# FFN input product of a two-layer decoder trunk: four instead of three seven-product blocks per layer, with three of four weight sums made by accumulating DMAs

## The chip, the cores and the metric

One NeuronCore of a Trainium2 chip runs the whole program: two layers over 256 tokens of width 1024, batch 1. The metric is the device time of one execution in microseconds (us), lower is better. Engines are named as in the profile: PE (matmul), PEld (its weight load), DVE (vector), ACT (scalar), POOL, and SP, which only issues DMAs.

## What is computed

Only the feed-forward part of each layer (SwiGLU) is touched. D_MODEL is 1024, FFN_HIDDEN is 2816, all data is float32.

```python
    h = rms_norm(x, ffn_norm)
    gate, up = jnp.split(h @ w_ffn_in, 2, axis=-1)
    return x + (jax.nn.silu(gate) * up) @ w_ffn_out
```

## The kernel before

**Float32 on PE.** Each weight tile `raw` of 128x2048 floats (1 MB, loaded as two DMAs of 512 KB from `wpk`) is split into a high part `wh` (ACT copy to fp32r, in `high`) and a low part `wl` = raw - wh (DVE, in `low`). The activations are split the same way. `mm3` then makes one float32 product of three matmuls of 128x512: high by high, high by low, low by high.

**Slabs.** The FFN's 2816 hidden columns are 11 slabs of 256. Slabs 0 and 1 run first (`slab`). The rest of a layer follows the table `FFN`: `("D", 2), ("Q", 3), ("D", 5), ("Q", 6), ("D", 8), ("Q", 9)`. "D" is one slab by `dense`: 2 weight tiles, 48 matmuls of 512 columns, for both token tiles. "Q" is two slabs by `quad`, a block of seven products in Winograd's form of Strassen's scheme: the two token tiles and the two halves of the 1024 input channels make a 2x2 block matrix of activations; the gate and up columns and the same two channel halves make a 2x2 block matrix of weights 11, 12, 21, 22 (one raw tile each). Seven products of 12 matmuls replace eight. Their operands are sums: S1 to S4 of activations, made once per layer by `quarter_sums`, and T1 to T4 of weights, made for every quad by `difference`, one DVE instruction of 128x2048 each (line 172):

```python
T1 = B12 - B11;  T2 = B22 - T1;  T3 = B22 - B12;  T4 = B21 - T2
```

T1 overwrites the tile of 11, T3 the tile of 12, T2 and T4 share a tile of their own (`T2..q`). PSUM bank qX collects 11, T2, T1 in turn; qY, qV, qZ take 21, 22, T3 and T4.

**The second FFN product.** Each slab's hidden values (256 columns) are transposed (`hidden_T`, tiles `aTT`) and multiplied by one weight tile "fo" (24 matmuls, `fo_all`). Two fo units stand inside each quad, one after each dense slab but the first.

**Order.** `unit_order` makes one list of weight tiles: a quad is the tuple `PRODUCTS` = 11, 21, 22, fo, T2, T3, T1, fo, T4. PE runs it in this order. After each unit, `ahead` calls `staged`, which emits the high part of the unit LOOK = 4 places ahead, the low part of the one 3 ahead, and the weight sum of the one 5 ahead. So ACT and DVE work in a fixed order, some four units before PE. There are 4 raw tiles (`RAWS`), 4 pairs wh, wl (`RING`), and one extra tile (tag `yT`) that takes weight 22 early. All loads are issued by SP, in an order that the scheduler fixes at build time; a load waits until its raw tile is released. POOL issues no load here and does nothing from the end of the layer's constants to the next norm. `later(d, f)` runs `f` after d more units ("ticks"); QUAD_AT sets d for a quad's transposes.

Of the kernel before, what the change touches and what calls it, by code (L numbers as in the profile page):

```python
# [18 lines left out]
P = 128  # L19
# [27 lines left out]
A_AT, B_AT = (1, 8), (1, 3)  # L47
QK_T, IX_T, SC_AT = 4, 4, 1
MT_AT, FI_AT = 3, 3
QUAD_AT = (3, 3)  # L50
WO = ((0, 0, 0), (0, 1, 0), (0, 0, 1), (1, 0, 0), (1, 1, 0), (0, 1, 1), (1, 0, 1), (1, 1, 1))
FFN = (("D", 2), ("Q", 3), ("D", 5), ("Q", 6), ("D", 8), ("Q", 9))
LOOK = 4
PRODUCTS = ("11", "21", "22", "fo", "T2", "T3", "T1", "fo", "T4")
LOADED = {"11": "11", "T1": "12", "21": "21", "22": "22"}
FRONT = ("gA0", "ix")
BLOCKS = ("ak", "aq", "av", "bk", "gA1", "bq", "bv", "gB0", "uA", "gB1", "uB")
# [28 lines left out]
def tile_trunk(ctx, tc, x, angle, wpk, widx, gnorm, gbias, gqk, dlam, subln, const, out):  # L86
# [15 lines left out]
    def b8(shape, name, dt=F32):  # L102
        return pp.tile(shape, dt, name=name, tag="b8", bufs=5)
# [54 lines left out]
    stage = {}  # L158
    diffs = {}

    def difference(n):
        l, name, i = seq[n]
        if n + 1 < len(seq) and seq[n + 1][2] == "T2":
            l, name, i = seq[n + 1][:2] + ("T1",)
        elif name[0] != "q" or i == "T1":
            return
        D = diffs.setdefault((l, name), {})

        def less(new, a, b, to=None):
            a, b = [D[x] if x[0] == "T" else raw_of((l, name, x)) for x in (a, b)]  # L170
            to = {"a": a, "b": b}[to] if to else b8([P, 2048], f"T2{l}{name}")
            nc.vector.tensor_tensor(to, a, b, ALU.subtract)
            D[new] = to

        if i == "T1":
            less("T1", "12", "11", "b")
        elif i == "T2":
            less("T2", "22", "T1")
        elif i == "T3":
            less("T3", "22", "12", "b")  # L180
        elif i == "T4":
            less("T4", "21", "T2", "b")

    def high(n):
        u = seq[n]
        raw = diffs[u[:2]].pop(u[2]) if u[2] in ("T1", "T3", "T4") else diffs[u[:2]]["T2"] if u[2] == "T2" else raw_of(u)
        hi = new_ready(n)[0]
        m = 1 if u[1][0] == "q" and u[2][0] == "T" else 2
        w = 2048 // m
        for k in range(m):  # L190
            nc.scalar.activation(hi[:, k * w:k * w + w], raw[:, k * w:k * w + w], AF.Copy)  # L191
        if u[2] == "11":
            raw_of(u[:2] + ("21",)), raw_of(u[:2] + ("12",))
        stage["raw", n] = raw

    def low(n):
# [1 line left out]
        split[0] += 2  # L198

    def staged(k, end):  # L200
        for fn, m in ((high, k), (low, k - 1), (difference, k + 1)):
            n = max(stage.get(fn, 0), split[0] // 2)
            while n <= min(m, end):
                fn(n)
                n += 1
            stage[fn] = n
# [115 lines left out]
    def quarter_sums(N, banks):  # L322
        name = N["name"]
        f1, f2 = N["f"]
        tiles = [b8([P, 4, 4, P], f"{name}S{h}", F32R) for h in "hl"]
        N["S"] = [[a[:, i] for a in tiles] for i in range(4)]
        s1, s2, s3, s4 = [t2k([P, 512], f"{name}s{i}") for i in range(4)]
        nc.scalar.activation(s4, banks[1], AF.Copy)
        nc.vector.tensor_tensor(s1, banks[0], s4, ALU.add)
        nc.vector.tensor_tensor(s3, f1, banks[0], ALU.subtract)  # L330
        nc.vector.tensor_tensor(s2, s1, f1, ALU.subtract)
        nc.vector.tensor_tensor(s4, f2, s2, ALU.subtract)
        for i, v in ((0, s1), (3, s4), (1, s2), (2, s3)):
            hilo(*N["S"][i], heads(v, 4))

# [415 lines left out]
    for l in range(DEPTH):  # L751
# [195 lines left out]
        def quad(s):  # L947
# [22 lines left out]
            def plus(to, p):  # L970
                return lambda: nc.vector.tensor_tensor(to, to, p, ALU.add)

            def added(to, a, p):
                return lambda: nc.vector.tensor_tensor(to, a, p, ALU.add)

            def silu(t):
                return lambda: nc.scalar.activation(G[t], G[t], AF.Silu)

            def gated(t):
                def f():  # L980
                    nc.vector.tensor_tensor(U[t], G[t], U[t], ALU.mult)
                    later(QUAD_AT[t], lambda: hidden_T(s, t, U[t], range(4)))
                return f

            X = bank(f"qX{name}")
            product(X, A(0, 0), "11", True, [copied(G[0], X)])
            Y = bank(f"qY{name}")
            product(Y, A(0, 1), "21", True, [plus(G[0], Y), silu(0)])
            V = bank(f"qV{name}")
            product(V, S4, "22", True)  # L990
            fo_all()
            product(X, S2, "T2", False, [copied(G[1], X)])
            Z = bank(f"qZ{name}")
# [104 lines left out]
```

## Time and profile before

| | us |
|---|---|
| median of 3 runs (765.39 to 765.80) | 765.46 |
| the profiled execution | 765.12 |
| its span, first to last instruction | 763.4 |
| PE busy | 753.9 (99%) |
| DVE busy | 611.1 (80%) |
| ACT busy | 469.0 (61%) |
| POOL busy | 79.7 (10%) |
| DMA queue q1 (SP's loads), share of 16 engines | 49.6% |
| read from HBM | 136.11 MB |

The FFN of layer 0 lies at about 206 to 400 us, that of layer 1 at about 581 to 760 us. The granted TensorE clock is 1.00 throughout, the 2.4 GHz level. The durations of matmuls in the profile overlap, since PE pipelines them: what one costs is the distance between two starts.

### The profile page before, as it was taken

How to read it: one execution, taken by the hardware profiler on the slowest of the kernel's cores; microseconds unless marked ns; L12 is line 12 of the kernel's file. 1: busy time of each engine (PE TensorE's matmuls, PEld its weight loads, DVE VectorE, ACT ScalarE, POOL GpSimd, SP SyncE). 2: the span in 40 equal slices, each digit the busy share in tenths (PEclk: the TensorE clock that was granted, in tenths of full speed). 3: DMA queues.
4: the chain of work that ended last, by engine and by line, in shares of the span. 5: the costliest groups of instructions: out<-in, count | busy, mean ns of one | idle time of the engine just before them, and what ended most of it. 6: DMA issues, size and time to landing. Idle time of an engine off the chain costs nothing.

```text
span 763.4 us, 10187 instructions
## 1 busy us (share of the span) xinstructions
PE 753.9 (99%) x3638; PEld 617.3 (81%) x3638; DVE 611.1 (80%) x907; ACT 469.0 (61%) x938; POOL 79.7 (10%) x103
## 2 busy tenths in 40 slices
PE   8999999999999999999999999999999999999998
PEld 5878887888888788888888787888888887888886
DVE  4899858768677979979868987667777799797993
ACT  4766596655665655656437676876546656565560
POOL 4741220010030000000011401200001000000000
PEclk9999999999999999999999999999999999999999
DMA  9744635436532752816755273453475227367141
GB/s 302 288 183 166 234 113 181 173 115 231 199 115 104 267 229 110 329 57 224 248 192 221 76 255 125 169 177 124 166 265 205 110 96 280 121 234 263 55 166 55
DMA packets 40452, 137.81 MB, mean 181 GB/s; under 512 B 4897, under 2 KB 5665, under 8 KB 40402
## 3 DMA queue, kind: packets, MB, share of 16 engines
q1 hardware_dynamic: 40320, 136.97, 49.6%
q8 instruction: 28, 0.46, 0.2%
q0 software_dynamic: 80, 0.20, 0.1%
q14 instruction: 22, 0.18, 0.1%
q10 hardware_dynamic: 2, 0.00, 0.0%
HBM read 136.11 MB, written 1.05 MB: 180 GB/s over the span
## 4 chain that ended last, share of the span: by engine, by line
PE 86%; DVE 7%; POOL 2%; issue 2%; DMA 1%; ACT 1%; SPq 0%; ACTq 0%; DVEq 0%
PE fi L238 5%; PE fi L236 5%; PE fi L237 5%; PE fo L237 5%; PE fo L238 5%; PE fo L236 5%; DVE wl L197 3%; PE gB L236 2%; PE gB L238 2%; PE wo L238 2%; PE wo L236 2%; PE gB L237 2%; PE wo L237 2%; PE qX L238 2%; PE qX L237 2%
## 5 line engine op out<-in xcount | busy, mean ns | idle before, releaser
L236 PE MATMUL fo<-wh,aTh 128*128 128x512 f32 (+1 forms) x100 | 38.3, 383 | 0.0
L238 PE MATMUL fo<-wh,aTl 128*128 128x512 f32 (+1 forms) x100 | 38.1, 381 | 0.0
L237 PE MATMUL fo<-wl,aTh 128*128 128x512 f32 (+1 forms) x100 | 38.1, 381 | 0.0
L197 DVE TENSOR_TENSOR wl<-raw1q,wh 128x2048 fp32r<-128x2048 f32 x15 | 34.0, 2284 | 0.6 <-ACT wh L191 0.6
L197 DVE TENSOR_TENSOR wl<-raw0q,wh 128x2048 fp32r<-128x2048 f32 x15 | 34.0, 2284 | 0.6 <-ACT wh L191 0.6
L237 PE MATMUL fo<-wl,aT 128*128 128x512 f32 x80 | 31.4, 392 | 0.6 <-DVE wl L197 0.6
L236 PE MATMUL fi<-wh,f0Th 128*128 128x512 f32 x80 | 31.8, 398 | 0.0
L236 PE MATMUL fi<-wh,f1Th 128*128 128x512 f32 x80 | 31.7, 397 | 0.0
L236 PE MATMUL fo<-wh,aT 128*128 128x512 f32 x80 | 31.5, 394 | 0.0
L238 PE MATMUL fo<-wh,aT 128*128 128x512 f32 x80 | 31.2, 390 | 0.0
L238 PE MATMUL fi<-wh,f0Tl 128*128 128x512 f32 x80 | 31.2, 390 | 0.0
L238 PE MATMUL fi<-wh,f1Tl 128*128 128x512 f32 x80 | 31.2, 390 | 0.0
L237 PE MATMUL fi<-wl,f1Th 128*128 128x512 f32 x80 | 31.2, 390 | 0.0
L237 PE MATMUL fi<-wl,f0Th 128*128 128x512 f32 x80 | 31.1, 389 | 0.0
L191 ACT ACTIVATE wh<-raw0q 128x1024 fp32r<-128x1024 f32 (+1 forms) x24 | 29.1, 1264 | 0.5 <-ACT wh L191 0.5
L191 ACT ACTIVATE wh<-raw1q 128x1024 fp32r<-128x1024 f32 (+1 forms) x24 | 29.1, 1264 | 0.5 <-ACT wh L191 0.5
L191 ACT ACTIVATE wh<-raw1fo 128x1024 fp32r<-128x1024 f32 x22 | 22.1, 1052 | 11.3 <-PE fo L238 6.3
L191 ACT ACTIVATE wh<-raw0fo 128x1024 fp32r<-128x1024 f32 x22 | 22.1, 1052 | 11.1 <-PE fo L238 6.4
L236 PE MATMUL wo<-wh,mTh 128*128 128x512 f32 x64 | 25.6, 400 | 0.0
L197 DVE TENSOR_TENSOR wl<-raw1fo,wh 128x2048 fp32r<-128x2048 f32 x11 | 25.0, 2284 | 0.0
L197 DVE TENSOR_TENSOR wl<-raw0fo,wh 128x2048 fp32r<-128x2048 f32 x11 | 25.0, 2283 | 0.0
L238 PE MATMUL wo<-wh,mTl 128*128 128x512 f32 x64 | 25.0, 391 | 0.0
(1060 smaller groups left out, 2505.0 us busy)
## 6 DMA issues: line engine op xcount, KB each, us to landing
raw0q<-wpk SPq DMA_DIRECT2D x24, 512.0 KB, 5.0
raw1q<-wpk SPq DMA_DIRECT2D x24, 512.0 KB, 5.0
raw0fo<-wpk SPq DMA_DIRECT2D x22, 512.0 KB, 4.6
raw1fo<-wpk SPq DMA_DIRECT2D x22, 512.0 KB, 4.2
raw0fi<-wpk SPq DMA_DIRECT2D x20, 512.0 KB, 4.2
raw1fi<-wpk SPq DMA_DIRECT2D x20, 512.0 KB, 4.1
raw0gA<-wpk SPq DMA_DIRECT2D x8, 512.0 KB, 6.2
raw0gB<-wpk SPq DMA_DIRECT2D x8, 512.0 KB, 4.2
```

The lines of the kernel that those rows point to most:

```text
L191: nc.scalar.activation(hi[:, k * w:k * w + w], raw[:, k * w:k * w + w], AF.Copy)
L197: nc.vector.tensor_tensor(ready[n][1], stage.pop(("raw", n)), ready[n][0].bitcast(F32), ALU.subtract)
L236: nc.tensor.matmul(acc, lhsT=sh, rhs=mh, start=first, stop=False, skip_group_check=more)
L237: nc.tensor.matmul(acc, lhsT=sh, rhs=ml, start=False, stop=False, skip_group_check=more)
L238: nc.tensor.matmul(acc, lhsT=sl, rhs=mh, start=False, stop=last, skip_group_check=more)
```

## The change

The table `FFN` has one dense slab (2) and four quads (3, 5, 7, 9). The quad's signs are turned round so that the weight sums are plain additions: T3 = 12 + 22, T2 = T3 + 11, T1 = 11 + 12, T4 = T2 + 21. The activation sums and the last steps of the quad take the minus signs (`scalar_tensor_tensor` in place of `tensor_tensor`). Of the four sums only T2 stays on DVE. The others are accumulating DMAs, issued by POOL (`more`): the addend is read from HBM and added onto a tile that lies in SBUF, T3 onto the tile of 12, T1 onto the tile of 11, T4 onto the tile of T2, each in two DMAs of 512 KB. The raw tile of 21 is then needed only for its own product, that of 22 too, and 12 has no raw use but T3. Product 22 moves to the end of the quad and accumulates onto qX; bank qV and the DVE step `added` are gone.

```diff
-QUAD_AT = (3, 3)
+QUAD_AT = (3, 2)
...
-FFN = (("D", 2), ("Q", 3), ("D", 5), ("Q", 6), ("D", 8), ("Q", 9))
+FFN = (("D", 2), ("Q", 3), ("Q", 5), ("Q", 7), ("Q", 9))
 LOOK = 4
-PRODUCTS = ("11", "21", "22", "fo", "T2", "T3", "T1", "fo", "T4")
+ADDED = ("q3", "q5", "q7", "q9")
+PRODUCTS = ("11", "21", "fo", "T2", "T3", "T1", "fo", "T4", "22")
...
-        if i == "T1":
-            less("T1", "12", "11", "b")
-        elif i == "T2":
-            less("T2", "22", "T1")
-        elif i == "T3":
-            less("T3", "22", "12", "b")
-        elif i == "T4":
-            less("T4", "21", "T2", "b")
+    def more(to, l, name, x):
+        src, w = where[l, name, x]
+        for j in range(2):
+            nc.gpsimd.dma_start(to[:, j * w:j * w + w], src[j], accum_op=ALU.add)
...
+        if i == "11":
+            D["T3"] = B("12")
+            more(D["T3"], l, name, "22")
+        elif i == "21":
+            D["T2"] = D["T4"] = b8([P, 2048], f"T2{l}{name}")
+            nc.vector.tensor_tensor(D["T2"], D["T3"], B("11"), ALU.add)
+        elif i == "T2":
+            D["T1"] = B("11")
+            more(D["T1"], l, name, "12")
+        elif i == "T1":
+            if name in ADDED:
+                more(D["T4"], l, name, "21")
+            else:
+                nc.vector.tensor_tensor(D["T4"], D["T4"], B("21"), ALU.add)
...
-        nc.vector.tensor_tensor(s1, banks[0], s4, ALU.add)
+        nc.vector.tensor_tensor(s1, s4, banks[0], ALU.subtract)
         nc.vector.tensor_tensor(s3, f1, banks[0], ALU.subtract)
-        nc.vector.tensor_tensor(s2, s1, f1, ALU.subtract)
-        nc.vector.tensor_tensor(s4, f2, s2, ALU.subtract)
+        nc.vector.scalar_tensor_tensor(s2, s1, -1.0, f1, ALU.mult, ALU.subtract)
+        nc.vector.scalar_tensor_tensor(s4, f2, -1.0, s2, ALU.mult, ALU.subtract)
...
-            def gated(t):
+            def gated(t, up):
                 def f():
-                    nc.vector.tensor_tensor(U[t], G[t], U[t], ALU.mult)
-                    later(QUAD_AT[t], lambda: hidden_T(s, t, U[t], range(4)))
+                    nc.vector.scalar_tensor_tensor(U[t], up, -1.0, G[t], ALU.mult, ALU.mult)
+                    later(QUAD_AT[t] - (s + 2 == NFO and t == 0), lambda: hidden_T(s, t, U[t], range(4)))
...
-            V = bank(f"qV{name}")
-            product(V, S4, "22", True)
             fo_all()
...
-            product(X, S1, "T1", False, [copied(U[1], X), added(U[0], U[1], V), gated(0), plus(U[1], Z)])
+            product(X, S1, "T1", False, [copied(U[1], X), plus(U[1], Z)])
             fo_all()
-            product(Z, A(1, 1), "T4", False, [plus(G[1], Z), silu(1), gated(1)])
+            product(Z, A(1, 1), "T4", False, [plus(G[1], Z), silu(1), gated(1, U[1])])
+            product(X, S4, "22", False, [gated(0, X)])
```

How this moves instructions is shown at three places. In the names, `wh` and `wl` are the split weights, `raw0q` a raw tile of a quad in layer 0, `raw0fo` and `raw0fi` those of the second product and of a dense slab, `T20q` the tile of T2 and T4, `g` and `u` the gate and up values, `aT` and `aTl` low parts of transposed hidden values.

DVE, layer 0, the last quad (slabs 9 and 10) of the kernel before, from the low part of 22 to the low part of T4; raw0q_3047 is 22, raw0q_2963 holds T1, raw0q_2973 is 12 and then T3, raw0q_2970 is 21:

```order
L197 TENSOR_TENSOR wl_3051<-raw0q_3047,wh_3050 128x2048
L172 TENSOR_TENSOR T20q_3082<-raw0q_3047,raw0q_2963 128x2048
L276 TENSOR_TENSOR aT_3099<-aTT_3096,aT_3099 128x256
L197 TENSOR_TENSOR wl_3078<-raw0fo_3074,wh_3077 128x2048
L172 TENSOR_TENSOR raw0q_2973<-raw0q_3047,raw0q_2973 128x2048
L971 TENSOR_TENSOR g_3102<-g_3102,qY_3125 128x512
L197 TENSOR_TENSOR wl_3121<-T20q_3082,wh_3120 128x2048
L197 TENSOR_TENSOR wl_3141<-raw0q_2973,wh_3140 128x2048
L197 TENSOR_TENSOR wl_3158<-raw0q_2963,wh_3157 128x2048
L172 TENSOR_TENSOR T20q_3082<-raw0q_2970,T20q_3082 128x2048
L197 TENSOR_TENSOR wl_3177<-raw0fo_3173,wh_3176 128x2048
L197 TENSOR_TENSOR wl_3208<-T20q_3082,wh_3207 128x2048
```

DVE after the change, in the quad of slabs 7 and 8, from the low part of T2 to the T2 sum of the next quad; raw0q_2750 holds T3, raw0q_2769 T1, raw0q_2976 is 22:

```order
L201 TENSOR_TENSOR wl_2859<-T20q_2777,wh_2858 128x2048
L975 TENSOR_TENSOR g_2862<-g_2862,qY_2886 128x512
L280 TENSOR_TENSOR aTl_2907<-aTT_2901,aTh_2906 128x512
L201 TENSOR_TENSOR wl_2881<-raw0q_2750,wh_2880 128x2048
L201 TENSOR_TENSOR wl_2911<-raw0q_2769,wh_2910 128x2048
L201 TENSOR_TENSOR wl_2930<-raw0fo_2926,wh_2929 128x2048
L201 TENSOR_TENSOR wl_2960<-T20q_2777,wh_2959 128x2048
L975 TENSOR_TENSOR u_2865<-u_2865,qZ_2963 128x512
L201 TENSOR_TENSOR wl_2980<-raw0q_2976,wh_2979 128x2048
L180 TENSOR_TENSOR T20q_3011<-raw0q_2984,raw0q_3003 128x2048
```

The rows of line 172 between the low parts are gone but for one, which makes the next quad's T2 (line 180); it now stands behind the low part of 22, and it reads a tile (raw0q_2984) that a DMA of POOL has to finish first.

POOL before, end of the constants for layer 1 and the start of the next norm:

```order
L428 TENSOR_TENSOR sg_2059<-gq_2051,plain 128x5x32 x2
L425 TENSOR_TENSOR cg_2063<-gq_2051,plain 128x320
L428 TENSOR_TENSOR sg_2064<-gq_2051,plain 128x5x32 x2
L271 TENSOR_SCALAR a1r_3382<-a1ss_3366 128x1
L272 TENSOR_TENSOR a1r_3382<-a1r_3382,mhalf 128x1
L271 TENSOR_SCALAR a1r_3432<-a1ss_3402 128x1
```

POOL after, two quads of layer 0 and the start of the next norm:

```order
L165 DMA raw0q_2750<-wpk 128x1024 x2
L165 DMA raw0q_2769<-wpk 128x1024 x2
L165 DMA T20q_2777<-wpk 128x1024 x2
L165 DMA raw0q_2984<-wpk 128x1024 x2
L165 DMA raw0q_3003<-wpk 128x1024 x2
L165 DMA T20q_3011<-wpk 128x1024 x2
L275 TENSOR_SCALAR a1r_3387<-a1ss_3371 128x1
L276 TENSOR_TENSOR a1r_3387<-a1r_3387,mhalf 128x1
```

Each of the new rows is one sum, T3, T1 and T4 in turn; T4's pair (T20q_2777) is followed directly by T3's pair of the next quad (raw0q_2984).

SP before, loads from the second quad of layer 0 (11, 21, 12, two fo) to the next dense slab, with the third quad's 22 (raw0q_3047) ahead of it:

```order
L129 DMA raw0q_2614<-wpk 128x1024 x2
L129 DMA raw0q_2621<-wpk 128x1024 x2
L129 DMA raw0q_2624<-wpk 128x1024 x2
L129 DMA raw0fo_2725<-wpk 128x1024 x2
L129 DMA raw0fo_2824<-wpk 128x1024 x2
L129 DMA raw0q_3047<-wpk 128x1024 x2
L129 DMA raw0fi_2875<-wpk 128x1024 x2
L129 DMA raw0fi_2899<-wpk 128x1024 x2
```

SP after, from the 22 of the second quad (raw0q_2742) over the third quad's 12, 11, 21 and fo to its 22:

```order
L130 DMA raw0q_2742<-wpk 128x1024 x2
L130 DMA raw0fo_2692<-wpk 128x1024 x2
L130 DMA raw0q_2750<-wpk 128x1024 x2
L130 DMA raw0q_2769<-wpk 128x1024 x2
L130 DMA raw0q_2791<-wpk 128x1024 x2
L130 DMA raw0fo_2826<-wpk 128x1024 x2
L130 DMA raw0q_2976<-wpk 128x1024 x2
```

The loads of dense slabs between the quads are gone; quads follow each other with four raw tiles and two fo tiles each, and 12 comes first.

## Rows read from the trace of the kernel before

**Rows 1.** The page, part 1: span, busy us (share), instructions.
```profile
span 763.4 us, 10187 instructions
...
PE 753.9 (99%) x3638; PEld 617.3 (81%) x3638; DVE 611.1 (80%) x907; ACT 469.0 (61%) x938; POOL 79.7 (10%) x103
```

**Rows 2.** Busy time by stretch: two quads of layer 0, then its FFN.
```profile
core 0: us, PE busy (x) PEld busy (x) DVE busy (x) ACT busy (x) POOL busy (x), PEclk, DMA share, GB/s
236.00:264.00 28.00, 27.99 (x124) 22.42 (x123) 26.49 (x17) 16.39 (x19) 0.00 (x0) 1.00 0.39 141
290.00:312.00 22.00, 22.00 (x100) 18.25 (x99) 21.69 (x12) 14.63 (x14) 0.00 (x0) 1.00 0.54 199
...
202.00:380.00 178.00, 177.68 (x810) 146.06 (x809) 155.54 (x124) 108.59 (x132) 6.01 (x9) 1.00 0.51 185
```

**Rows 3.** Timeline of PE, first and last of 36 matmuls without a gap: start, duration.
```profile
206.26 0.39 PE L236 MATMUL fi<-wh,f0Th 128*128 128x512 f32 x1
...
214.19 0.39 PE L238 MATMUL fi<-wh,f0Tl 128*128 128x512 f32 x1
```

**Rows 4.** Timeline of PE, the fo unit in the first quad, layer 0, then layer 1.
```profile
263.60 0.39 PE L236 MATMUL fo<-wh,aT 128*128 128x512 f32 x1
264.30 0.50 PE L237 MATMUL fo<-wl,aT 128*128 128x512 f32 x1 [0.31 <-DVE wl L197]
...
638.91 0.50 PE L237 MATMUL fo<-wl,aT 128*128 128x512 f32 x1 [0.31 <-DVE wl L197]
```

**Rows 5.** Timeline of DVE at the same place.
```profile
261.96 2.28 DVE L197 TENSOR_TENSOR wl<-raw0fo,wh 128x2048 fp32r<-128x2048 f32 x1
264.17 2.28 DVE L197 TENSOR_TENSOR wl<-T20q,wh 128x2048 fp32r<-128x2048 f32 x1
266.46 0.69 DVE L974 TENSOR_TENSOR u<-u,qV 128x512 f32<-128x512 f32 x1
```

**Rows 6.** Groups of DVE by shape, 214 to 383 us: form, count | busy us, mean ns.
```profile
L197 DVE TENSOR_TENSOR wl<-raw0q,wh 128x2048 fp32r<-128x2048 f32 x15 | 34.0, 2284 | 0.6 <-ACT wh L191 0.6
...
L172 DVE TENSOR_TENSOR raw0q<-raw0q,raw0q 128x2048 f32<-128x2048 f32 x6 | 13.7, 2283 | 0.0
...
L172 DVE TENSOR_TENSOR T20q<-raw0q,T20q 128x2048 f32<-128x2048 f32 x3 | 6.9, 2284 | 0.0
```

**Rows 7.** The same view for ACT.
```profile
L191 ACT ACTIVATE wh<-raw0q 128x1024 fp32r<-128x1024 f32 x18 | 18.0, 1051 | 0.5 <-ACT wh L191 0.5
...
L191 ACT ACTIVATE wh<-raw0q 128x2048 fp32r<-128x2048 f32 x6 | 11.1, 1903 | 0.0
```

**Rows 8.** Timeline of PE: the same transpose in the first and second quad.
```profile
269.65 0.27 PE L245 MATMUL aTT<-cst,u 128*128 128x128 f32 x1
...
317.36 0.27 PE L245 MATMUL aTT<-cst,u 128*128 128x128 f32 x1
```

**Rows 9.** DMA, 214 to 383 us: queue (packets, MB, share), issues (KB, us to landing).
```profile
q1 hardware_dynamic: 9031, 31.18, 50.4%
...
raw0fo<-wpk SPq DMA_DIRECT2D x22, 512.0 KB, 4.6
raw0q<-wpk SPq DMA_DIRECT2D x18, 512.0 KB, 5.0
```

**Rows 10.** DMA, first 30 us: the queue of SP, and two loads of 128 KB.
```profile
q1 hardware_dynamic: 3451, 9.23, 88.9%
...
cst<-const POOLq DMA_DIRECT2D x1, 128.0 KB, 5.4
dl<-dlam SPq DMA_DIRECT2D x1, 128.0 KB, 4.1
```

**Rows 11.** Timeline of POOL: a DMA issue, and the first instruction after the FFN.
```profile
1.26 0.79 POOL L351 DMA_DIRECT2D cst<-const  x1 [0.43 <-issue]
...
381.42 0.30 POOL L271 TENSOR_SCALAR a1r<-a1ss 128x1 f32<-128x1 f32 x1 [162.31 <-ACT junk L293]
```

More of the change, by code (lines that the diff above doesn't have):

```diff
@@ L159, in tile_trunk, with sums, B @@
     diffs = {}
-    def difference(n):
+    def more(to, l, name, x):
+        src, w = where[l, name, x]
+        for j in range(2):
+            nc.gpsimd.dma_start(to[:, j * w:j * w + w], src[j], accum_op=ALU.add)
+    def sums(n):
         l, name, i = seq[n]
[L163 to L166, printed above, removed]
         D = diffs.setdefault((l, name), {})
[L169 to L173, printed above, removed]
-        if i == "T1":
-            less("T1", "12", "11", "b")
-        elif i == "T2":
-            less("T2", "22", "T1")
-        elif i == "T3":
-            less("T3", "22", "12", "b")
-        elif i == "T4":
-            less("T4", "21", "T2", "b")
+        def B(x):
+            return raw_of((l, name, x))
+        if i == "11":
[4 more added lines that the diff above has]
+            nc.vector.tensor_tensor(D["T2"], D["T3"], B("11"), ALU.add)
+        elif i == "T2":
+            D["T1"] = B("11")
[5 more added lines that the diff above has]
+                nc.vector.tensor_tensor(D["T4"], D["T4"], B("21"), ALU.add)
     def high(n):
         u = seq[n]
-        raw = diffs[u[:2]].pop(u[2]) if u[2] in ("T1", "T3", "T4") else diffs[u[:2]]["T2"] if u[2] == "T2" else raw_of(u)
+        raw = diffs[u[:2]][u[2]] if str(u[2])[0] == "T" else raw_of(u)
         hi = new_ready(n)[0]
@@ L191, in high @@
             nc.scalar.activation(hi[:, k * w:k * w + w], raw[:, k * w:k * w + w], AF.Copy)
-        if u[2] == "11":
-            raw_of(u[:2] + ("21",)), raw_of(u[:2] + ("12",))
         stage["raw", n] = raw
@@ L200, in staged @@
     def staged(k, end):
-        for fn, m in ((high, k), (low, k - 1), (difference, k + 1)):
+        for fn, m in ((high, k), (low, k - 1), (sums, k + 1)):
             n = max(stage.get(fn, 0), split[0] // 2)
@@ L971, in plus @@
                 return lambda: nc.vector.tensor_tensor(to, to, p, ALU.add)
-            def added(to, a, p):
-                return lambda: nc.vector.tensor_tensor(to, a, p, ALU.add)
             def silu(t):
                 return lambda: nc.scalar.activation(G[t], G[t], AF.Silu)
-            def gated(t):
+            def gated(t, up):
                 def f():
-                    nc.vector.tensor_tensor(U[t], G[t], U[t], ALU.mult)
-                    later(QUAD_AT[t], lambda: hidden_T(s, t, U[t], range(4)))
+                    nc.vector.scalar_tensor_tensor(U[t], up, -1.0, G[t], ALU.mult, ALU.mult)
+                    later(QUAD_AT[t] - (s + 2 == NFO and t == 0), lambda: hidden_T(s, t, U[t], range(4)))
                 return f
```

## The prediction

> **What bounds the kernel now.** I read the page's part 1 first: PE is busy 753.9 of 763.4 us [rows 1], so only what shortens PE's own stream, or makes it wait, can move the time. The windows say the same of the FFN alone: 177.68 of 178.0 us in layer 0, at granted clock 1.00 [rows 2]. A trap lies in the profile's durations. A matmul of 128x512 shows 0.39 us, but 36 of them without a gap start from 206.26 to 214.19, so one costs (214.19 - 206.26) / 35 = 0.2266 us [rows 3].
>
> PE's one loss in an FFN's quads is in the first quad of each layer. There two matmuls of an fo unit start 0.70 us apart instead of 0.23, because DVE's low part wl came late; layer 1 shows the same wait of 0.31 us in the same place [rows 4]. DVE is why: two starts of its 128x2048 instruction lie 2.21 us apart (261.96 and 264.17) [rows 5], and in the quads it is busy 26.49 of 28 and 21.69 of 22 us [rows 2]. So inside a quad DVE is the next bound, right behind PE; the dense slabs in between let it recover. POOL is idle for 162 us of an FFN [rows 11], and the DMA engines work half the time [rows 2, 9].
>
> **PE's work.** Per layer, two dense slabs (96 matmuls) become one quad (84). The hidden transposes stay at 8. Two layers save 24 matmuls: 24 x 0.2266 = 5.44 us, all on PE's stream.
>
> A quad with its two fo units is 84 + 48 = 132 matmuls, 29.9 us. The old period of quad, dense slab and three fo units was 317.36 - 269.65 = 47.71 us [rows 8] for 204 matmuls (46.2 us) and 12 transposes, so one transpose costs PE about 0.12 us and a new quad with its 8 lasts 30.9 us. Four stand back to back, with no dense slab to recover in. That is what every other engine has to keep up with.
>
> **DVE.** Before, one period held 12 low parts and 4 sums, 16 x 2.21 = 35.4 us, and 8 short instructions of the quad at 0.6 to 0.69 (5.2 us), 85% of 47.71 before the dense slab's own short ones. The twelve sums per layer are the groups of six, three and three at line 172, at 2283 ns each like the low parts [rows 6]. Now a quad holds 9 low parts and one sum, 22.1 us, and 7 short ones (one, `added`, goes), 4.8 us: 26.9 of 30.9 us, 87%. With all four sums it would have been 33.5, over the period; so the adds on DMA carry the change. Where DVE failed, the first quad, T1's sum, T3's and T4's are gone from ahead of the late low part: 6.6 us off a lateness of 0.31. I therefore count both stalls as gone, 264.30 - 263.60 - 0.23 = 0.47 us each, 0.94 in all; if they stay, add that back. The turned signs put two `scalar_tensor_tensor` in each layer's activation sums and two in each quad, in place of as many instructions of the same shape: nothing, under PE's matmuls.
>
> **ACT.** Five high parts in halves at 2 x 1.05 us and four whole ones at 1.90 [rows 7] are 18.1 us per quad, and seven short ones at 0.6 make 22.3 of 30.9, 72%: hidden.
>
> **The adds.** 24 sums of 1 MB become 48 DMAs of 512 KB on POOL. No row before shows a DMA that adds, so I bound one from both sides. In 214 to 383 us SP's queue took 50.4% of 169 us for 31.18 MB, 2.73 us per MB, or 1.43 us of all 16 engines per 512 KB [rows 9]. That is the low end: an add that costs what a load costs. The high end is twice that, 2.87 us, since an add has to fetch the tile that it adds onto as well as the addend. In latency a load takes 4.6 to 5.0 us to land [rows 9]; in the first 30 us a load of 128 KB from POOL landed in 5.4 where SP's took 4.1 [rows 10], and POOL spent 0.79 us to issue one [rows 11], so I add 1.3 us for the queue, and the pair lands about 0.8 + 5.0 + 1.3 = 7.1 us after its issue where nothing is in its way.
>
> Per quad, six raw tiles (four of the quad, two fo) are 6.29 MB, 17.2 us of the engines. Three added tiles take 8.6 us at the low end, 25.8 of 30.9 in all (83%); at the high end 17.2, 34.4 in all (111%). Break-even is (30.9 - 17.2) / 6 = 2.28 us per add, 1.6 times a load. The engines can be held near full: in the first 30 us the same queue had 88.9% of them at 26.7 / 9.23 = 2.89 us per MB [rows 10].
>
> Who waits for them: T2's sum on DVE now waits for T3's add, and behind it stand the low parts of 11 and 21; ACT's high part of T4 waits for T4's add, and behind it stand the copy out of qX and the high part of 22; POOL's queue is in order, so T4's pair stands right ahead of the next quad's T3 pair. That is the tightest place. It opens when the low part of T2 is made, at PE's product 11, and closes when the next T2 sum is due, at PE's product T1: 21, fo, T2, T3, T1, or 72 matmuls, 16.3 us. In it fall four adds and three loaded tiles (fo, 12, 11): 10 x 1.43 = 14.3 us at the low end, 4 x 2.87 + 8.6 = 20.1 at the high end. A late T2 sum has cover: PE needs the low part of 11 only after fo, T4 and 22, 48 matmuls or 10.9 us later, of which DVE needs 4.4 for the sum and the low part. T4's high part has 21, fo and T2, 10.9 us, against 7.1.
>
> I take the low end, or near it: what the engines are busy with in a load is moving 4 KB rows into the tile, and an add writes no more rows than a load, while the fetch of the tile goes the other way. It is a choice, not a reading, and it carries the forecast.
>
> The Trainium skill speaks against it. Its page "Collectives: The Full Stack", section "The bandwidth ceiling: the fold count and why AG ≠ RS ≠ AR", says that an add in the DMA engines costs no time in itself, but needs two source reads on one queue and so halves the rate. By that rule an add would be at my high end; no row of this trace has such a DMA to test it.
>
> **Sum.** The profiled execution took 765.12 us, its span 763.4 plus 1.7 around it. 765.12 - 5.44 - 0.94 = 758.7. The median of the runs stands 0.34 above the profiled one: **759.1 us**, 0.8% faster. This case's own range is 758.3 to 761.5, with the stalls kept or a few short waits at its upper end.
>
> **Rivals.** (A) *The DMA engines become the bound, and it is slower.* If an add costs 2.87 us, each quad wants 34.4 us of transfers in 30.9, 3.5 us short, and the tight place is 3.8 short. The first quad of a layer has most of its tiles loaded before, and the cover of about 6.5 us delays the stall, but the shortage comes back with every quad; six quads at 3.6 are 22 us: 781. It decides from 2.28 us per add on. For it: an add must read its target. Against it: DMA share is only half now, and reads and writes need not share a limit. By the rule of the Trainium skill's "Collectives: The Full Stack" quoted above, this is the outcome. (B) *Latency takes the gain back.* The adds have throughput, but a pair behind SP's loads takes over 10.9 us, ACT stands at T4's high part, and PE loses 0.7 to 0.9 us in each of the eight quads: 759.1 + 8 x 0.8 = 765.5, no change. For it: the chain T3, T2, T1 and T2, T4 runs through three queues in order. Against it: four units of lookahead. (C) *DVE is still late*, 87% busy with no dense slab between: the two stalls stay, 760.0, inside the forecast's range.
>
> **How the numbers follow.** Forecast with C 0.66, A 0.20, B 0.10, and 0.04 for what I have not thought of, half on each side. About 0.2%, 1.5 us, is what a measurement of this kernel can tell from no change. Faster: 0.66 and 0.02, and 0.02 of B's lower edge, 0.70. Same: the rest of B, 0.08. Slower: A and 0.02, 0.22. The range runs from 758.3 to 772: it holds the forecast, B and the near edge of A, and leaves out the body of A.
>
> **What would show it.** Right: PE has 24 fewer matmuls, no wait of its own in the quads above 0.3 us, DVE's line 172 groups give way to one of four per layer, DMA share in the quads 0.8 to 0.9, an add's pair lands in 7 to 10 us. Wrong: PE waiting in every quad, from the second on, for a low part of T4 or 11, with DVE or ACT waiting for a POOL DMA before it, DMA share at 0.95 or more there (A) or well below (B).

## The result, and the profile after

The changed kernel takes **769.52 us** (median of 5 runs, 768.28 to 770.66) beside 765.39 of the kernel before in the same comparison: ratio 1.0061, 95% interval 1.0050 to 1.0072. It is 0.6% slower where 0.8% faster was forecast. The time lies inside the range of 758.3 to 772, but by luck: that end of the range was drawn for the near edge of rival A, and neither the forecast nor A's 781 came. The profiled execution took 768.28 us.

The page, span and part 1, and the two queues of part 3 (packets, MB, share of 16 engines):

```profile
span 766.5 us, 10291 instructions
...
PE 749.3 (98%) x3614; PEld 613.5 (80%) x3614; DVE 589.0 (77%) x889; ACT 482.7 (63%) x940; POOL 122.0 (16%) x151
...
q1 hardware_dynamic: 40320, 136.97, 48.2%
q0 software_dynamic: 6992, 25.37, 18.0%
```

Against [rows 1], PE has 24 instructions less, as forecast, and 4.6 us less of busy time, but the span is 3.1 us longer: PE now stands idle for 17.2 us of it instead of 9.5. The windows of the quads of layer 0 show where (busy us of PE, PEld, DVE, ACT, POOL; granted clock, DMA share, GB/s):

```profile
236.00:264.00 28.00, 28.00 (x126) 23.05 (x125) 20.82 (x15) 17.67 (x20) 4.32 (x5) 1.00 0.94 238
264.00:290.00 26.00, 26.00 (x120) 21.37 (x119) 21.74 (x15) 15.76 (x16) 5.24 (x6) 1.00 1.02 293
290.00:321.00 31.00, 28.90 (x125) 23.51 (x124) 25.27 (x17) 20.66 (x21) 5.24 (x6) 0.94 0.98 284
321.00:352.00 31.00, 30.04 (x137) 24.61 (x136) 25.26 (x17) 20.79 (x21) 3.51 (x4) 1.00 0.98 287
```

The DMA share went from 0.39 and 0.54 [rows 2] to 0.94 and more. PE's first loss comes after 290 us, not in the first quad, where the 0.31 us waits of [rows 4] are gone. Whom PE, ACT and DVE wait for, from the waits (us in total, times, longest; PE's of the whole execution, the other two of 214 to 383 us):

```profile
PE aTT L249 <- DVE u L982: 7.4, 4, 2.8
...
DVE wl L201 <- ACT wh L197: 15.7, 6, 4.3
ACT wh L197 <- DMA T20q<-wpk: 11.0, 4, 3.7
```

In the quads PE waits for no weight part. It waits at the hidden transposes (aTT) for a gated u. One such case, followed through four engines in the timeline (start, duration, engine, instruction; in brackets the idle time before it and what ended it; `T20q` holds T2 and then T4):

```profile
279.33 1.76 POOL L165 DMA_DIRECT2D T20q<-wpk  x2 [8.03 <-DVE wl L201]
...
286.11 0.60 ACT L972 ACTIVATE g<-qX 128x512 f32<-128x512 f32 x1 [0.66 <-PE qX L242]
290.25 1.92 ACT L197 ACTIVATE wh<-T20q 128x2048 fp32r<-128x2048 f32 x1 [3.54 <-DMA T20q<-wpk]
...
292.19 2.29 DVE L201 TENSOR_TENSOR wl<-T20q,wh 128x2048 fp32r<-128x2048 f32 x1 [4.08 <-ACT wh L197]
...
303.74 0.69 DVE L982 SCALAR_TENSOR_TENSOR u<-u,g 128x512 f32<-128x512 f32 x1 [0.70 <-ACT g L978]
...
304.49 0.66 PE L249 MATMUL aTT<-cst,u 128*128 128x128 f32 x4 [2.10 <-DVE u L982]
```

T4's pair of adds is issued at 279.33. ACT comes to T4's high part at 290.25 - 3.54 = 286.71, 7.4 us later, and the tile is ready 10.9 us after the issue. DVE stands behind ACT for 4.08 us, and in the 12 us to the gated u it has only 1.2 us of idle time left; 2.1 us of the delay reach PE. The transfers of the same stretch, 214 to 383 us (queues, then issues with the median us to landing):

```profile
q1 hardware_dynamic: 8986, 31.14, 48.2%
q0 software_dynamic: 3456, 12.58, 40.5%
...
raw0q<-wpk SPq DMA_DIRECT2D x26, 512.0 KB, 7.1
...
T20q<-wpk POOLq DMA_DIRECT2D x8, 512.0 KB, 8.3
```

Adds (q0): 0.405 x 169 / 12.58 = 5.44 us of all engines per MB, 2.85 us per add of 512 KB (0.524 MB). Loads (q1): 0.482 x 169 / 31.14 = 2.62 us per MB. An add costs 2.1 times a load. The first pair of a layer, alone on the engines in 219 to 226 us, says the same:

```profile
q0 software_dynamic: 274, 1.05, 83.8%
...
raw0q<-wpk POOLq DMA_DIRECT2D x2, 512.0 KB, 6.3
```

0.838 x 7 = 5.9 us for the pair, 2.93 per add, and 6.3 us from the issue of an add to its landing (the median of the two) with nothing in its way, where the prediction had counted 7.1.

### The profile page after: what moved, and what is told of

It is laid out like the page before. It is cut to its first block, busy times and chain, and to the rows that moved or that the text cites. A ratio compares the mean times of both kernels' runs of the same rounds, so it can differ in the third digit from the quotient of the medians.

```text
span 766.5 us, 10291 instructions
## 1 busy us (share of the span) xinstructions
PE 749.3 (98%) x3614; PEld 613.5 (80%) x3614; DVE 589.0 (77%) x889; ACT 482.7 (63%) x940; POOL 122.0 (16%) x151
## 4 chain that ended last, share of the span: by engine, by line
PE 71%; DMA 12%; DVE 8%; issue 3%; POOL 3%; ACT 2%; SPq 0%; DVEq 0%; ACTq 0%; POOLq 0%
DMA raw0q<-wpk 5%; DMA raw1q<-wpk 5%; PE fo L242 3%; PE fo L240 3%; PE fo L241 3%; PE qX L242 2%; PE qX L241 2%; PE qX L240 2%; PE fi L242 2%; PE fi L240 2%; PE fi L241 2%; PE gB L240 2%; PE gB L242 2%; PE gB L241 2%; DVE wl L201 2%
## 5 line engine op out<-in xcount | busy, mean ns | idle before, releaser
L240 PE MATMUL fo<-wh,aTh 128*128 128x512 f32 (+1 forms) x132 | 51.4, 389 | 0.0
L242 PE MATMUL fo<-wh,aTl 128*128 128x512 f32 (+1 forms) x132 | 50.7, 384 | 0.0
L201 DVE TENSOR_TENSOR wl<-T21q,wh 128x2048 fp32r<-128x2048 f32 x8 | 18.3, 2287 | 14.1 <-ACT wh L197 14.1
L201 DVE TENSOR_TENSOR wl<-T20q,wh 128x2048 fp32r<-128x2048 f32 x8 | 18.3, 2287 | 13.8 <-ACT wh L197 13.8
L242 PEld LDWEIGHTS fo<-wh,aTl 128*128 128x128 f32 x132 | 24.8, 188 | 5.1
L241 PEld LDWEIGHTS fo<-wl,aTh 128*128 128x128 f32 x132 | 24.8, 188 | 4.7
L240 PEld LDWEIGHTS fo<-wh,aTh 128*128 128x128 f32 x132 | 24.8, 188 | 4.5
L165 POOL DMA_DIRECT2D raw1q<-wpk x16 | 14.8, 1067 | 79.7 <-DVE wl L201 73.3
L165 POOL DMA_DIRECT2D raw0q<-wpk x16 | 14.8, 1082 | 72.8 <-DVE wl L201 53.6
L241 PE MATMUL wo<-wl,mTh 128*128 128x512 f32 x64 | 25.0, 390 | 0.0
```

What stands on the lines that cost most here:

```text
L165: nc.gpsimd.dma_start(to[:, j * w:j * w + w], src[j], accum_op=ALU.add)
L201: nc.vector.tensor_tensor(ready[n][1], stage.pop(("raw", n)), ready[n][0].bitcast(F32), ALU.subtract)
L240: nc.tensor.matmul(acc, lhsT=sh, rhs=mh, start=first, stop=False, skip_group_check=more)
L241: nc.tensor.matmul(acc, lhsT=sh, rhs=ml, start=False, stop=False, skip_group_check=more)
L242: nc.tensor.matmul(acc, lhsT=sl, rhs=mh, start=False, stop=last, skip_group_check=more)
```

## The experiments

Names used in the expectations: **P**, the price: an add holds the DMA engines for twice a load; **L**, the latency of POOL's queue and of the chain T3, T2, T4; **V**, DVE and ACT too late without a dense slab; **PL**, formed later: the price works through T4's tile, which becomes ready too late in its chain. Every ratio is to the kernel before in the same comparison.

**e1_plain_loads.** The adds become loads, so the sums T3, T1 and T4 are left out.

```diff
-            nc.gpsimd.dma_start(to[:, j * w:j * w + w], src[j], accum_op=ALU.add)
+            nc.gpsimd.dma_start(to[:, j * w:j * w + w], src[j])
```

> The accumulate is taken off the 48 DMAs of POOL: each now overwrites its tile with the addend, so the three weight sums are left out (T1, T3 and T4 are one tile each), with the same issues, waits and bytes from HBM. Theory P (price: an add keeps the 16 DMA engines busy twice as long as a load, 2.9 us per 512 KB against 1.4, and the quads ran at a share of 0.98 to 1.02): the quad needs 25.8 us of transfers in 30.9, T4's pair lands earlier, PE's 7.4 us of waits go, about 759 us. Theory L (latency: POOL's queue and its chain of waits, whatever is moved): the waits stay, 767 to 770. Theory V (DVE and ACT too late with no dense slab between quads, whatever DMA does): the waits stay too.

757.70 us (0.9911, 0.9898 to 0.9924). DMA, 214 to 383 us:

```profile
q0 software_dynamic: 3456, 12.58, 20.6%
...
T20q<-wpk POOLq DMA_DIRECT2D x8, 512.0 KB, 4.5
```

The same bytes at half the time, 2.77 us per MB, and a T4 tile after 4.5 instead of 8.3 us. No PE wait is left in the quads. A quad lasts 30.9 us, as worked out (T4's pairs are issued at 278.45, 309.33 and 340.19). So PE's, DVE's and ACT's parts of the forecast hold in these quads (V falls), as does POOL's queue by itself (L falls); what the adds cost is 769.5 - 757.7 = 11.8 us.

**e2_t4_on_dve.** T4's sum on DVE.

```diff
-ADDED = ("q3", "q5", "q7", "q9")
+ADDED = ()
```

> T4's sum goes back to DVE (ADDED empty); T3 and T1 stay adds. Theory P: per quad 17.2 + 4 x 2.9 = 28.8 us of transfers in 30.9, share about 0.93; DVE gets 2.2 us more, 29.1 of 30.9. ACT no longer waits for T4's pair, PE's waits at the hidden transposes shrink from 7.4 to 0 to 3 us, 760 to 764 us. Theory V: DVE at 94% is worse, 770 or more. Theory L: T3's and T1's chain remains, 765 to 768.

763.90 us (0.9989, 0.9980 to 0.9998). The engines' share in 264 to 352 us is 0.86, and PE still waits for u, shorter, but longer than the 0 to 3 us that P allowed:

```profile
PE aTT L249 <- DVE u L982: 4.9, 6, 1.0
```

**e3_transposes_later.** All adds, the hidden transposes one or two slots later.

```diff
-QUAD_AT = (3, 2)
+QUAD_AT = (4, 4)
...
-                    later(QUAD_AT[t] - (s + 2 == NFO and t == 0), lambda: hidden_T(s, t, U[t], range(4)))
+                    later(2 if s + 2 == NFO else QUAD_AT[t], lambda: hidden_T(s, t, U[t], range(4)))
```

> The hidden transposes of a quad, where PE waited, are moved one or two units later (d = 4, 4 instead of 3, 2; the last quad of a layer keeps 2, 2); the adds stay as they are. If PE only waited there because the last steps of the quad come 2 to 3 us late (a lateness that is passed on but does not grow), the waits go and the gain shows: 758 to 761. If the DMA engines are short by 3.5 us per quad and the lateness adds up, it comes out at the weight parts instead: 764 to 770, with PE waiting for wl of T4, 11 or 21.

767.48 us (1.0037, 1.0024 to 1.0050). The wait goes from the transposes to product 21's low part:

```profile
PE qY L241 <- DVE wl L201: 4.0, 4, 1.2
...
PE aTT L249 <- DVE u L982: 0.6, 1, 0.6
```

More slack at the place where PE waits gives little: DVE's lost time comes out one product further on. That is the branch that the expectation had named for engines that are short in every quad.

**e4_dense_between.** Three quads per layer with the dense slabs between, as before, and the adds.

```diff
-FFN = (("D", 2), ("Q", 3), ("Q", 5), ("Q", 7), ("Q", 9))
+FFN = (("D", 2), ("Q", 3), ("D", 5), ("Q", 6), ("D", 8), ("Q", 9))
...
-ADDED = ("q3", "q5", "q7", "q9")
+ADDED = ("q3", "q6", "q9")
```

> The adds alone: slabs as before the change (three quads, dense slabs between), with the three sums by DMA. PE's work is that of before. Theory P: a period of 47.7 us holds 9 tiles of loads and 3 of adds, 25.8 + 17.2 = 43 us, share 0.9: no waits in the quads, and the two stalls of 0.47 us in the first quads go with DVE's relief: 764 to 765. Theory L: adds land too late in any arrangement, 766 to 770.

762.82 us (0.9974, 0.9965 to 0.9983), no PE wait in the quads, share 0.91 in 264 to 352 us. With time between them, adds at the high price are covered. It is 1.2 us faster than P's range; that rest has no row.

**e5_t4_on_dve_later** is e2 and e3 together; **e7_t4_first_quad_added** gives the adds back to the first quad of a layer.

```diff
-ADDED = ()
+ADDED = ("q3",)
```

> T4's sums on DVE (as in e2_t4_on_dve) and the hidden transposes one slot later in every quad but the last (as in e3_transposes_later). P (an add occupies the DMA engines twice as long as a load): with a third fewer adds the engines are 85 to 87% busy, as in e2, and the gated u is only a little late, 4.9 us of waits at the transposes in e2, the longest 1.0; one slot of three products later (2.7 us) covers them all: 763.9 - 4.9 = 759.0, between 758.5 and 760. Had e2's waits another cause, DVE's own load (78.9 of 88 us) as in V, they would move to the weight parts, as those of e3 did: 761 to 763.5.

> As e5_t4_on_dve_later, but T4's sum of the first quad of each layer stays with the DMAs (two more adds of 512 KB per layer) and DVE has one sum of 2.2 us less there. P: the first quad's tiles are loaded ahead, before the FFN's matmuls begin, so its shortage comes last, but what it adds to the queue, 5.8 us of engines per layer, is taken from the next quads, which are at 85 to 87%: no PE wait comes of it and the time is that of e5 within 0.7 us. If DVE's load is what still costs e5 something: 0.5 to 1.5 us faster than e5. If the engines have no room even here: 1 to 2 us slower than e5.

e5: 760.24 us (0.9945, 0.9933 to 0.9956), 0.2 above P's range, e7: 760.00 us (0.9944, 0.9930 to 0.9957). With a share of 0.88 in e5 the later transposes do cover the waits for u, unlike in e3; 0.5 us of waits for weight parts are left. Why both stay 2.3 us or more above e1 isn't settled.

**e6_loads_and_copies**, **e8_copies_ahead**, **e10_copies_between.** Plain loads as in e1, and with each pair two copies of 512 KB from HBM to a spare place in HBM, which nobody waits for. Only the order of the four differs: load, copy, load, copy; copy, copy, load, load; load, copy, copy, load. e10's lines:

```diff
         for j in range(2):
+            nc.gpsimd.dma_start(to[:, j * w:j * w + w], src[j])
+            for k in range(2 - 2 * j):
+                nc.gpsimd.dma_start(spare[spared[0]], src[k])
+                spared[0] += 1
```

> Kernel e1_plain_loads (the 48 adds are plain loads, so that the sums T3, T1 and T4 are left out and the output is not the reference's) with one more transfer behind each of the 48: a copy of the same 512 KB from HBM to a spare place in HBM that nothing reads and nothing waits for. No DMA adds anything here, but POOL's queue holds the DMA engines about as long as it does with the adds, if a copy from HBM to HBM costs what a load costs (2.6 us per MB; no row shows one, the run's own queue row will say). P (it is the time of the engines alone): the time of e1, 757.7, goes back to that of the changed kernel, 769.5, between 766 and 773, with the DMA share in the quads at 0.95 or more and PE waiting at the hidden transposes for u. If something else in an add were to blame, its own latency or its exclusive hold of the tile: it stays at 757.5 to 760. If the copies turn out far cheaper or dearer than loads, the share decides what is to be read.

> Kernel e6_loads_and_copies with each pair's two copies put ahead of its two loads instead of each behind its own (sums left out as there, so the output is not the reference's). The bytes and the engines' time are the same as in e6; what changes is that a tile is ready only when its copies and its loads are both through, which is when an add's pair would be ready (some 1.7 us later still, since POOL issues two more DMAs first, at 0.87 us each). Theory PL (what costs is that the tile itself is ready twice the engine time after its issue, with the engines near full): ACT's waits for T4's tile, 4.5 us in e6's first layer against 11.0 in the changed kernel, come back to 9 or more, PE waits at the hidden transposes for u, 765 to 773. Theory P as stated for e6 (the engines' time alone, wherever it falls): the same time as e6, 760.2, within 1.5.

> Kernel e6_loads_and_copies with the order of the four DMAs of a pair changed: load of the first half, both copies, load of the second half (sums left out as there, so the output is not the reference's). In e8_copies_ahead the copies waited for nothing, so they ran ahead of the place in time at which an add may start; here the first load waits for the tile, and the copies and the second load stand behind it in POOL's queue, so that the extra engine time falls where an add's falls and the tile is ready only behind it. PL (the tile ready late by twice the engine time, at the place where an add stands): ACT's waits for T4's tile 9 us or more in layer 0, PE waits at the hidden transposes for u, 763 to 771. If engine time and its place do not matter and it is a property of the adding transfer that no load and no copy has: 757.5 to 760.5, as e6 and e8.

e6: 760.18 us (0.9943, 0.9922 to 0.9964). e8: 757.86 us (0.9913, 0.9899 to 0.9927). e10: **769.23 us** (1.0059, 1.0045 to 1.0072), the changed kernel's time without a single add. The windows of 264 to 352 us, of e6, e8 and e10 in turn:

```profile
264.00:352.00 88.00, 86.27 (x392) 70.89 (x391) 73.67 (x48) 59.19 (x59) 16.92 (x32) 1.00 1.00 393
```

```profile
264.00:352.00 88.00, 88.00 (x401) 72.89 (x400) 76.73 (x50) 60.77 (x60) 15.64 (x30) 1.00 1.01 397
```

```profile
264.00:352.00 88.00, 82.14 (x373) 67.16 (x372) 70.83 (x48) 55.54 (x56) 16.64 (x32) 1.00 0.96 374
```

The share is about the same, and highest where nothing is lost. So P as e6's expectation put it (the engines' time alone, wherever it falls) fell, and e8 seemed to take PL with it. The timeline of POOL tells why it did not. In e8:

```profile
271.03 0.99 POOL L168 DMA_DIRECT2D spare<-wpk  x2
280.06 1.09 POOL L171 DMA_DIRECT2D T20q<-wpk  x2 [8.04 <-DVE wl L207]
281.15 0.99 POOL L168 DMA_DIRECT2D spare<-wpk  x2
284.08 0.56 POOL L171 DMA_DIRECT2D raw0q<-wpk  x1 [1.94 <-issue]
```

The copies meant for one pair wait for nothing and run right behind the pair before it: T4's at 271.03, 9 us ahead of its loads, those of the next pair at 281.15. e8 had not put the cost where an add has it, and e6 half of it (one copy ahead of a tile's second half; ACT waits 4.5 us for T4's tile in layer 0). In e10 the first load holds the copies back, and the second half of the tile stands behind them (POOL's rows, then the waits, ACT's of 214 to 383 us, PE's of the whole execution):

```profile
279.33 0.55 POOL L168 DMA_DIRECT2D T20q<-wpk  x1 [7.71 <-DVE wl L207]
279.86 0.98 POOL L170 DMA_DIRECT2D spare<-wpk  x2
280.84 0.57 POOL L168 DMA_DIRECT2D T20q<-wpk  x1
```

```profile
ACT wh L203 <- DMA T20q<-wpk: 12.2, 4, 4.1
...
PE aTT L255 <- DVE u L988: 9.7, 5, 3.2
```

ACT's waits for T4's tile come back (12.2 us, 11.0 in the changed kernel), and PE's for u with them. So no adding is needed for a loss of this size, and the share alone doesn't make it: tiles that are ready late do. By the waits it is T4's; T3's and T1's are delayed in the same way, so the time by itself doesn't single it out. One reserve: a load and a copy together hold the engines nearly as long as an add (the queue's share in 214 to 383 us is 38.1% in e10, 40.5% in the changed kernel), but 374 to 397 GB/s moved in these runs where the changed kernel moved 288, so a share near 1 doesn't say that nothing more could pass.

**e9_t4_on_pool.** As e5, T4's sum on POOL.

```diff
-                nc.vector.tensor_tensor(D["T4"], D["T4"], B("21"), ALU.add)
+                nc.gpsimd.tensor_tensor(D["T4"], D["T4"], B("21"), ALU.add)
```

> As e5_t4_on_dve_later, but T4's sum is made by POOL's own tensor_tensor instead of DVE. The only rows of POOL's are small: 0.80 us for 160 elements per partition and 1.03 for 320, so by their slope 1.03 + 1728 x 0.00144 = 3.5 us for 2048, against DVE's 2.2. PL and P: the DMA engines have room as in e5 (two adds per quad), DVE has 2.2 us less per quad; PE's small waits of e5 for weight parts (0.5 us in all) go: 758.2 to 760, as e5 or up to 1.5 us faster. If POOL and DVE hinder each other while POOL's sum runs, DVE's instructions beside it grow over 2.3 us and it is 761 or more.

779.62 us (1.0194, 1.0180 to 1.0208): the forecast missed by 20 us, and the branch for POOL and DVE hindering each other came. POOL's timeline:

```profile
246.69 4.63 POOL L188 TENSOR_TENSOR T20q<-T20q,raw0q 128x2048 f32<-128x2048 f32 x1 [10.72 <-PE aTT L249]
```

4.63 us and not 3.5, and DVE's low parts of quad tiles took 2.75 us on the mean instead of 2.28 (from the groups of DVE). PE waited 14.2 us for weight parts.

**e11_t4_two_added.** As e7, with the last quad's T4 sum added by DMA too: `ADDED = ("q3", "q9")`.

> As e7_t4_first_quad_added, with T4's sum of the last quad of each layer given back to the DMAs as well; DVE keeps the two in the middle. The stretch behind the last quad has the DMA engines at 64% in e5 and e7, so there is room for 5.8 us more, but the last quad's transposes stay at two slots, so a late u shows there. If there is room in time too: as e7, 759 to 760.5; if T4's add is late in the last quad as in the changed kernel, where PE waited there: 760.5 to 763.

**759.75 us (0.9932, 0.9918 to 0.9945)**: it beats both kernels.

**e12_t4_last**, **e13_t4_last_later.** All adds; products 22 and T4 change places, on PE and so on ACT and DVE.

```diff
-PRODUCTS = ("11", "21", "fo", "T2", "T3", "T1", "fo", "T4", "22")
+PRODUCTS = ("11", "21", "fo", "T2", "T3", "T1", "fo", "22", "T4")
```

with `QUAD_AT = (3, 3)` in e12 and `(4, 4)` in e13, and two slots in the last quad. **e14_places_of_e12** keeps the order of the changed kernel and puts every transpose where e12 has it:

```diff
-QUAD_AT = (3, 2)
+QUAD_AT = (2, 4)
...
-                    later(QUAD_AT[t] - (s + 2 == NFO and t == 0), lambda: hidden_T(s, t, U[t], range(4)))
+                    later(QUAD_AT[t] - (s + 2 == NFO), lambda: hidden_T(s, t, U[t], range(4)))
```

> The changed kernel, all four added sums by DMA, with the products 22 and T4 of a quad in the other order: ACT's high part of 22 stands ahead of T4's, PE needs T4 one product (12 matmuls, 2.7 us) later, and the transposes of both halves come three slots after their product (two in the last quad). No byte and no DMA is changed, so the engines' time is that of the changed kernel. PL (the late T4 tile is the cause, and ACT standing at it while 22's tile lies ready): ACT's waits for T4's tile were 2 to 3.7 us in the four quads of layer 0, so 2.7 us more and 22's high part done meanwhile leave a wait of at most 1 us: 758.5 to 762, with the DMA share as high as before. If the shortage is one of the engines' throughput, as e3_transposes_later suggests, whose waits moved to the parts of 11 and 21: the wait comes out elsewhere and it is 765 to 769.

> As e12_t4_last with the transposes one slot later still (four; two in the last quad). PL: if e12 still waits at the transposes, this covers it: 758 to 761, and no slower than e12. Throughput: 765 to 769 with the waits at the weight parts.

> The changed kernel with its order of products (T4, then 22), but every hidden transpose at the place on PE that it has in e12_t4_last: behind product 11 of the next quad for the first half, behind 21 for the second. It tells apart the two things that e12 moved at once. PL as e12 was meant (ACT stands at T4's late tile, and DVE behind ACT): the waits of ACT for T4's tile stay at 10 to 15 us in layer 0, DVE still loses 3 to 4.6 us at T4's low part, PE's waits go from the transposes to the low parts of the next products as in e3_transposes_later: 765 to 769. If the places of the transposes made e12's gain: 761 to 763.5.

e12: **762.22 us** (0.9961, 0.9947 to 0.9974). e13: 765.79 us (1.0014, 1.0006 to 1.0023). e14: **773.77 us** (1.0113, 1.0098 to 1.0129). e12 is 0.2 us above PL's range. e12 and e14 have the same DMAs and the same places of the transposes, and are 11.6 us apart at a share of 1.00 and 0.99. e12, 264 to 352 us, and its waits (PE's of the whole execution, ACT's of 214 to 383 us, here and below):

```profile
264.00:352.00 88.00, 86.14 (x388) 70.19 (x387) 73.33 (x48) 58.80 (x59) 14.00 (x16) 1.00 1.00 288
...
ACT wh L197 <- DMA T20q<-wpk: 4.8, 2, 2.6
...
PE qX L241 <- DVE wl L201: 2.5, 3, 1.2
```

and e14's, with one of its waits in the last quad of layer 0:

```profile
264.00:352.00 88.00, 84.11 (x380) 68.44 (x379) 73.16 (x48) 56.88 (x57) 14.00 (x16) 1.00 0.99 287
...
ACT wh L197 <- DMA T20q<-wpk: 11.2, 4, 3.7
...
PE aTT L249 <- DVE u L982: 12.1, 7, 2.7
...
370.25 0.66 PE L249 MATMUL aTT<-cst,u 128*128 128x128 f32 x4 [2.25 <-DVE u L982]
```

In e12 ACT does 22's high part while T4's tile is still on its way, so it stands for 4.8 us instead of 11.2. But the 11.6 us are not the order of ACT's work alone. With 22 last, e14 has one product less than e12 between 22 and the transposes of the first half, which 22 completes, and none at all in the last quad of a layer, where PE stands there for 2.25 and 2.73 us. Its granted clock was lower too, 0.995 to 0.997 in its four runs against 0.999 to 1.000. So e14 missed twice: PE's waits stayed at the transposes, and the time is 4.8 us above its range.

e3 and e13 compare the orders better: both put the transposes of either half four slots after their product (two in the last quad). Their medians are 1.7 us apart (767.48 and 765.79), their profiled executions 0.75 the other way (765.70 and 766.45), though ACT's waits for T4's tile, e3 first, fall by 8.5 us:

```profile
ACT wh L197 <- DMA T20q<-wpk: 14.1, 4, 4.8
```

```profile
ACT wh L197 <- DMA T20q<-wpk: 5.6, 2, 3.1
```

e13 refuted "no slower than e12": 5.9 us of PE waits at weight parts instead of 3.6, and a time in the branch for throughput. Why later transposes cost here isn't settled, and how much of e12's gain on the changed kernel, 7.3 us, is the order and how much the places isn't either.

**e15_t4_last_two_added** is e12 with `ADDED = ("q3", "q9")`.

> e12_t4_last with T4's sum of the two middle quads of each layer on DVE, as in e11_t4_two_added: the order that gives T4 one product more, and 12.6 us per layer less of the engines' time. PL: what e12 still waits, 3.6 us in all at weight parts, goes with the lower share: 757.5 to 760, at least as fast as e11 (759.75). If DVE's extra 2.2 us in the middle quads, or the order itself, costs something: 760 to 762.

759.56 us (0.9939, 0.9926 to 0.9951): with e11 the fastest that computes everything, and not to be told from it.

## Why the prediction was wrong

**PE's work: right.** 24 matmuls went, and with loads in place of the adds the kernel took 757.7 where the sum gave 759.1; the 1.4 us between them have no row.

**The two stalls: right.** No wait stands in the first quads.

**The price of an add: wrong, and the step that carried the sign.** The low end, 1.43 us, was taken "as a choice, not a reading"; it measured 2.85 to 2.93, at the high end of 2.87. With 2.85 for 1.43 the prediction's own sum of a quad is 17.2 + 6 x 2.85 = 34.3 us in 30.9, and the gain of 6.4 us became a loss of 4.1. The argument for the low end, that an add writes no more rows than a load and that the fetch of the tile goes the other way, has nothing left. The rule of the Trainium skill's "Collectives: The Full Stack", section "The bandwidth ceiling: the fold count and why AG ≠ RS ≠ AR" (two source reads, half the rate), is stated there for a ReduceScatter. The trace of these adds agrees with it: 5.44 against 2.62 us per MB.

**Rival A: its price right, its time 12 us too long, its mechanism at most a part.** It made the loss out of throughput: some 3.6 us short in each of six quads, 22 us. By the measured prices a quad wants 6.29 x 2.62 + 3.15 x 5.44 = 33.6 us in 30.9, 2.7 short, and the middle quads of layer 0 do take about that long: T4's pairs are issued at 279.33, 312.52 and 346.18, 33.2 and 33.7 us apart (1.6 of the first by the clock, below). But e10 lost as much at a share of 0.96, without an add, and e12, with the same DMAs and the engines as full, is at 762.2, 4.5 us above e1. On the other side, e3 and e13 kept 9.8 and 8.1 us of loss over e1 with their waits moved to weight parts, as a shortage would have it. So throughput alone doesn't give the 11.8 us, and no run here divides them between the shortage and the late tile. A left out that the engines have slack ahead of the first quad (the share is 0.61 in 214 to 236 us of the changed kernel) and behind the last loads (0.76 in 352 to 383).

**Rival B: the place right, the size wrong.** "ACT stands at T4's high part, and PE loses" is what happened, but through the doubled price and not through latency at a load's price; e1 has the same queue and no wait. PE loses 1.0 to 2.8 us at four of eight quads, not 0.7 to 0.9 at each.

**The cover of T4: the second wrong step.** The 10.9 us were counted from PE's product 11, where the low part of T2 was to be made and T4's pair issued, to ACT's high part of T4 behind product T2. ACT did come there right behind product T2. But DVE makes the low part of T2 later, behind that of fo: product 11 ends at 274.56, where the first matmul of 21 starts, and the low part at 279.04.

```profile
274.56 0.39 PE L240 MATMUL qY<-wh,f0Th 128*128 128x512 f32 x1
...
276.76 2.28 DVE L201 TENSOR_TENSOR wl<-T20q,wh 128x2048 fp32r<-128x2048 f32 x1
```

That leaves 7.4 us from the issue to ACT, 0.3 over the 7.1 forecast, and the tile took 10.9; PE's product T4 itself never waited. The list of who stands behind the tile named the copy out of qX and 22's high part, but not DVE. DVE stood for 4.08 us behind ACT, and with 87% to do (which the prediction had) it didn't win that back within 12 us. What came late was the gated u, for which the prediction had no cover worked out at all. e10, which loses as much with such a late tile and no add, shows that this path is enough for a loss of this size.

**Rival C, DVE late by itself:** didn't come; DVE is busy 76.7 of 88 us in e1's quads (its window of 264 to 352 us), near the forecast 87%, and PE doesn't wait.

**"What would show it":** the share of 0.95 or more came true, as did waits of ACT, and of DVE behind it, for a DMA of POOL, but PE waiting in every quad for a low part of T4 or 11 didn't; the wait stood at the transposes.

The profiled executions of the changed kernel and of e1 are 768.28 - 757.89 = 10.4 us apart. Of these, 7.4 are PE's waits for u, and 1.6 a clock that fell behind the first of them (below); the other 1.4 have no row. The medians are 11.8 us apart, and the five runs of the changed kernel stand in the order of their mean granted clock: 768.28 at 0.998, 768.82 at 0.996, 769.52 and 770.06 at 0.995, 770.66 at 0.994. So the median run lost more by the clock than the profiled one.

## What to carry to other kernels

Price a new kind of transfer at its dearer bound until a run has shown it, and then don't stop at the share of the engines: two kernels with the same transfers (e8 and e10), at a share of 1.01 and 0.96, were 11.4 us apart, and the one with the higher share was the faster. Follow the tile to the first engine that takes it up in order, not only to the matmul that needs it last; count from when its issue can really start, and count what stands behind that engine. Here the second engine in the chain was near full, and what it lost stayed lost. Of the two ways out, taking some of the adds away (e11, 759.75, with later transposes) gained more than giving the late tile more time (e12, 762.2, where the order and the places of the transposes changed together), and both at once (e15, 759.56) no more than the first.

## What the runs showed of the hardware

An adding DMA from HBM into SBUF took 2.1 times the engines' time of a load (5.44 against 2.62 us per MB) and 0.88 us to issue on POOL (1.76 for the pair at 279.33), where a plain load there took 0.55 (e10's rows above).

PE's granted clock fell behind the 2.10 us wait in layer 0 of the changed kernel, once PE had started again. Windows and two matmul starts:

```profile
304.00:306.00 2.00, 1.51 (x9) 1.35 (x10) 2.00 (x2) 2.00 (x4) 0.49 (x1) 0.99 0.74 135
306.00:308.00 2.00, 2.00 (x7) 1.54 (x6) 2.00 (x4) 1.88 (x2) 0.00 (x0) 0.50 1.08 199
308.00:310.00 2.00, 2.00 (x7) 1.60 (x6) 2.00 (x2) 0.49 (x1) 0.00 (x0) 0.66 0.99 197
...
305.90 0.58 PE L241 MATMUL qX<-wl,f0Th 128*128 128x512 f32 x1
...
309.27 0.44 PE L240 MATMUL qY<-wh,f0Th 128*128 128x512 f32 x1
```

At 0.50, the 1.2 GHz level, the eight matmuls between these two starts take 309.27 - 305.90 = 3.37 us instead of 8 x 0.2266 = 1.81: 1.6 us on top of the wait. After the wait of 2.81 us in layer 1 the clock stayed at 1.00, so the length of a wait alone doesn't decide it; what does, no run here tells.

```profile
713.97 0.66 PE L249 MATMUL aTT<-cst,u 128*128 128x128 f32 x4 [2.81 <-DVE u L982]
...
716.00:718.00 2.00, 2.00 (x11) 1.65 (x10) 2.00 (x4) 1.98 (x3) 0.00 (x0) 1.00 1.10 207
```
